# The out-projection as one level of Strassen's block scheme, after all merges, with the sums of w_out blocks formed on chip

## The chip, the core and the metric

The kernel runs on one core of one Trainium2 chip. The metric is the device time of one execution in microseconds; the kernel before took 2602.24 us, the median of three runs (2600.22 to 2603.6).

## What is computed

One decoder layer on 1024 tokens and 16 learned meta tokens, model width 2048, all in float32. An input projection feeds an attention branch and a pooling branch, each 1024 wide. What the change touches is the end, after the branches' outputs stand in DRAM:

```python
y_attn = o_attn @ w_attn_up          # (tokens, 1024) @ (1024, 2048)
y_pool = o_pool @ w_pool_up
merged = sigmoid(m_attn) * y_attn + sigmoid(m_pool) * y_pool
hs = x + merged @ w_out              # (tokens, 2048) @ (2048, 2048)
return rmsnorm(hs, final_gain)[:, N_META:]
```

## The kernel before

Matmuls of float32 accuracy are made of three: an operand is split into a high part in the type float32r (ScalarE, L116) and the rest (VectorE, L117), and high x high, high x low and low x high are accumulated in PSUM (`mm3`, and L910 to L912 in the out-projection). A weight tile is always 128 x 512. `load_w` (L127) loads it through SyncE's queue (SP, L124) into one of four raw buffers `wr` and splits it into one of four pairs `wh`, `wl`. So a weight tile is loaded when the split of the fourth one before it has been done, and split when TensorE (PE) has finished with the fourth one before it.

The tokens are worked in two halves of 512 (`t`). For each half there is first a **merge**: for 16 blocks `c` of 128 output columns, `up_mm` multiplies pooled and attention outputs by the two up-projections (24 matmuls and two weight tiles each), VectorE multiplies by the gate (`sp` L895, `sa` L901), GpSimd (POOL) adds the two (L902), and the sum is split into `m`, which stays on chip. Then comes the **out-projection** of the half, `out_pass`: all 16 blocks of `m` against w_out, four token blocks `b` and column blocks `c` of 512; each weight tile serves 4 x 3 = 12 matmuls. Residual, squares and the final gain follow (L945 to L957), and the rows are stored. So the order of stages is merge 0, out 0, merge 1, out 1. The attention outputs of the second half are loaded and split during out 0 (`fill_o`), into the place of the first half's. The last 512 columns of out 1 go by halves of 256 columns per token block, from weights split ahead (`lw`).

Which instruction stands where in an engine's queue is not the program's order: a scheduler sets it when the kernel is built. Each engine then works through its own queue in order, SP through its DMA issues too: an issue that waits for a semaphore holds all issues behind it. Before the first merge stands the input projection, itself by a block scheme, whose sums GpSimd forms and SP stores (`d_r`, L245), and the attention.

Of the kernel before, what the change touches and what calls it, by code (L numbers as in the profile page):

```python
# [15 lines left out]
P = 128  # L16
# [56 lines left out]
def trunk_kernel(  # L73
# [779 lines left out]

    def o_quads():
        return xquads(0, HALF, xo) + xquads(1, HALF, xo)

    def m_quads():
        return xquads(2, HALF) + xquads(3, HALF, xc)

    o = o_quads()  # L860
    for n in range(WID // P):
        fill_o(o, 0, n)

    psB = ctx.enter_context(tc.tile_pool(name="psB", bufs=8, space=bass.MemoryType.PSUM, reuse_waits="tile"))
    pb = ctx.enter_context(tc.tile_pool(name="pb", bufs=2, side="right", reuse_waits="tile"))
# [4 lines left out]
    def up_mm(w, o, c):  # L870
        a = acc_b()
        for q in range(2):
            whi, wlo = load_w(w_src(w, q, c * P))
            for j in range(QD):
                k = slice(j * P, (j + 1) * P)
                mm3(a, whi[:, k], wlo[:, k], o[q][0][:, j], o[q][1][:, j], q + j == 0, q == 1 and j == QD - 1)
        return a

    def merge(t, o, m):
        order = [("p", 0), ("p", 1), ("p", 2)] if t == 0 else []  # L880
        for c in range(KC):
            if ("p", c) not in order:
                order.append(("p", c))
            order.append(("a", c))
        sps = {}
        cs = slice(t * HALF, (t + 1) * HALF)
        for n, (kind, c) in enumerate(order):
            if t == 0 and n < 3:
                for i in range(WID // P + 3 * n, WID // P + min(3 * n + 3, 8)):
                    fill_o(o, 0, i)  # L890
            if kind == "p":
                sp = pb.tile([P, HALF], F32, tag="sp", name=nm("sp"), bufs=3)
                nc.sync.dma_start(sp, d_sp[c][:, cs])
                a = up_mm(w_pu, o[:2], c)
                nc.vector.tensor_tensor(out=sp, in0=a, in1=sp, op=ALU.mult)  # L895
                sps[c] = sp
            else:
                sa = pb.tile([P, HALF], F32, tag="sa", name=nm("sa"))
                nc.sync.dma_start(sa, d_sa[c][:, cs])
                a = up_mm(w_au, o[2:], c)  # L900
# [13 lines left out]
    def out_pass(m, cs, done, extra=None):  # L914
        accs = {(c, b): acc_b() for c in cs for b in range(HB)}
        groups = [(0, 1)] + [(k,) for k in range(2, KC - 2)] + [(KC - 2, KC - 1)]
        for ks in groups:
            if extra is not None:
                for k in ks:
                    extra(k)  # L920
            ws = {(c, k): load_w(w_out[k * P : (k + 1) * P, c * 512 : (c + 1) * 512]) for k in ks for c in cs}
            for (c, b), a in accs.items():
                for k in ks:
                    out_mm(a, m, b, k, *ws[c, k])
# [115 lines left out]
```

## Time and profile before

| | |
|---|---|
| median of 3 runs | 2602.24 us |
| the profiled execution | 2601.93 us, of which its span 2600.2 us |
| granted TensorE clock, mean | 0.986 |
| merge 0 | from 1883.4 us |
| out-projection 0 | from 2060.1 us |
| last 512-column matmul of out 1 | 2545.4 us |
| half-wide matmuls of out 1 | 2545.6 to 2591.6 us |
| DMA moved | 415.88 MB, mean 160 GB/s |

Times within the profile are microseconds from the start of the span. A window's line gives its length, then busy time and number of instructions of PE matmul, PE weight load, VectorE (DVE), ScalarE (ACT) and GpSimd, then the granted clock of PE, the busy share of the 16 DMA engines and what they moved in GB/s. A matmul's row shows its whole passage through the array; the next one starts before it ends, so the rate is read from counts in a window. In a line of a tile, the three numbers are the least, median and greatest ns of one instruction.

### The profile page before, as it was taken

Reading aid. Unit: us, or ns where it says so; the run is one execution under the profiler, and the core shown is the slowest. Engines: PE = TensorE matmul, PEld = TensorE weight load, DVE = VectorE, ACT = ScalarE, POOL = GpSimd, SP = SyncE. Lnnn points to the kernel's source line nnn. Section 1 sums busy time; section 2 is a strip of 40 time slices with the busy share of each in tenths; the row PEclk is TensorE's granted clock in tenths of the full one; section 3 lists DMA queues with packets and bytes.
Section 4 is the critical chain, followed back from the end, with each engine's and each line's share of the span. In section 5 each row is a group of like instructions: output and inputs, shape, how many; then the busy total and the mean of one; then the engine's idle time right before and its main releaser. Section 6 shows DMA issues by size and latency. Waiting matters only on the chain.

```text
span 2600.2 us, 36248 instructions
## 1 busy us (share of the span) xinstructions
PE 2502.7 (96%) x12968; PEld 2132.8 (82%) x12968; DVE 1279.1 (49%) x2121; ACT 930.7 (36%) x1893; POOL 873.3 (34%) x794
## 2 busy tenths in 40 slices
PE   6898999999999999899999999999899999999998
PEld 5776788888888887888888888888688888788888
DVE  5442345443334444675576567656644334544432
ACT  6421222222222234224454545454532223322331
POOL 1655555554455444233323332333111100211010
PEclk9999999999999999999999999999999999999999
DMA  5566555665555567434434443433385434664421
GB/s 180 168 213 209 198 196 201 208 225 183 176 187 184 172 192 233 125 127 137 128 122 130 129 126 122 135 124 98 128 265 146 139 101 146 203 185 142 150 98 65
DMA packets 392054, 415.88 MB, mean 160 GB/s; under 512 B 29873, under 2 KB 264753, under 8 KB 390833
## 3 DMA queue, kind: packets, MB, share of 16 engines
q1 hardware_dynamic: 391872, 413.57, 49.8%
q8 instruction: 101, 1.65, 0.3%
q14 instruction: 81, 0.66, 0.1%
HBM read 302.62 MB, written 110.85 MB: 159 GB/s over the span
## 4 chain that ended last, share of the span: by engine, by line
PE 82%; DVE 5%; DMA 3%; POOL 3%; issue 1%; ACT 1%; SPq 0%; POOLq 0%; DVEq 0%; ACTq 0%
PE acc L138 17%; PE acc L140 17%; PE acc L139 17%; PE accb L912 4%; PE accb L911 4%; PE accb L910 4%; PE accb L140 4%; PE accb L138 4%; PE accb L139 4%; POOL r L236 2%; DMA raw<-in_w_in_dram 2%; PE tr L730 1%; DVE s L658 1%; DVE wl L117 1%; DVE bt L715 1%
## 5 line engine op out<-in xcount | busy, mean ns | idle before, releaser
L138 PE MATMUL acc<-x,wh 128*128 128x512 f32 (+2 forms) x2736 | 980.4, 359 | 26.3 <-ACT wh L116 18.3
L140 PE MATMUL acc<-x,wl 128*128 128x512 f32 (+2 forms) x2736 | 971.0, 355 | 4.9 <-DVE wl L117 3.6
L139 PE MATMUL acc<-x,wh 128*128 128x512 f32 (+2 forms) x2736 | 970.0, 355 | 0.0
L138 PEld LDWEIGHTS acc<-x,wh 128*128 128x128 f32 x2736 | 520.1, 190 | 96.6 <-ACT wh L116 22.4
L140 PEld LDWEIGHTS acc<-x,wl 128*128 128x128 f32 x2736 | 519.0, 190 | 81.1 <-DVE wl L117 8.9
L139 PEld LDWEIGHTS acc<-x,wh 128*128 128x128 f32 x2736 | 519.8, 190 | 63.1
L116 ACT ACTIVATE wh<-wr 128x512 fp32r<-128x512 f32 x480 | 302.4, 630 | 522.0 <-PE accb L139 162.8
L117 DVE TENSOR_TENSOR wl<-wr,wh 128x512 fp32r<-128x512 f32 x360 | 257.8, 717 | 277.8 <-ACT wh L116 266.1
L117 DVE TENSOR_TENSOR wl<-r,wh 128x512 fp32r<-128x512 f32 x160 | 151.7, 951 | 309.5 <-ACT wh L116 303.6
L117 POOL TENSOR_TENSOR wl<-wr,wh 128x512 fp32r<-128x512 f32 x120 | 167.3, 1394 | 343.6 <-ACT wh L116 287.0
L116 ACT ACTIVATE wh<-r 128x512 fp32r<-128x512 f32 x160 | 100.4, 632 | 457.1 <-POOL r L236 333.5
L236 POOL TENSOR_TENSOR r<-raw,raw 128x512 f32<-128x512 f32 x80 | 112.3, 1403 | 375.1 <-DMA raw<-in_w_in_dram 339.3
L236 POOL TENSOR_TENSOR r<-r,raw 128x512 f32<-128x512 f32 x160 | 221.0, 1382 | 12.2 <-DMA raw<-in_w_in_dram 2.3
L138 PE MATMUL accb<-x,wh 128*128 128x512 f32 x512 | 201.3, 393 | 9.0 <-ACT wh L116 9.0
L140 PE MATMUL accb<-x,wl 128*128 128x512 f32 x512 | 201.0, 393 | 3.0 <-DVE wl L117 3.0
L139 PE MATMUL accb<-x,wh 128*128 128x512 f32 x512 | 200.8, 392 | 0.0
L912 PE MATMUL accb<-wl,x 128*128 128x512 f32 x448 | 174.4, 389 | 1.0 <-DVE wl L117 1.0
L910 PE MATMUL accb<-wh,x 128*128 128x512 f32 x448 | 174.3, 389 | 0.0
L911 PE MATMUL accb<-wh,x 128*128 128x512 f32 x448 | 174.3, 389 | 0.0
L117 DVE TENSOR_TENSOR wl<-raw,wh 128x512 fp32r<-128x512 f32 x136 | 110.2, 819 | 116.3 <-ACT wh L116 116.3
L714 DVE TENSOR_TENSOR_SCAN wt<-wt 128x272 f32<-128x272 f32 (+5 forms) x128 | 107.7, 842 | 110.0 <-POOL wt L709 64.7
L902 POOL TENSOR_TENSOR sa<-sa,sp 128x512 f32<-128x512 f32 x32 | 50.9, 1590 | 324.8 <-DVE sa L901 324.8
(166 smaller groups left out, 3032.0 us busy)
## 6 DMA issues: line engine op xcount, KB each, us to landing
raw<-in_w_in_dram SPq DMA_DIRECT2D x96, 512.0 KB, 5.9
d_r<-r SPq DMA_DIRECT2D x160, 256.0 KB, 2.0
wr<-d_r SPq DMA_DIRECT2D x160, 256.0 KB, 2.9
raw<-in_w_in_dram SPq DMA_DIRECT2D x152, 256.0 KB, 5.1
wr<-in_w_out_dram SPq DMA_DIRECT2D x128, 256.0 KB, 2.6
wr<-in_w_in_dram SPq DMA_DIRECT2D x80, 256.0 KB, 3.0
wr<-in_w_pool_up_dram SPq DMA_DIRECT2D x64, 256.0 KB, 3.9
wr<-in_w_attn_up_dram SPq DMA_DIRECT2D x64, 256.0 KB, 3.4
```

What stands on the lines that cost most here:

```text
L116: nc.scalar.activation(hi, src, AF.Copy)
L117: (eng or nc.vector).tensor_tensor(out=lo, in0=src, in1=hi.bitcast(F32), op=ALU.subtract)
L138: nc.tensor.matmul(ps, wh, rh, start=first, stop=False, skip_group_check=skip)
L139: nc.tensor.matmul(ps, wh, rl, start=False, stop=False, skip_group_check=skip)
L140: nc.tensor.matmul(ps, wl, rh, start=False, stop=last, skip_group_check=skip)
L236: nc.gpsimd.tensor_tensor(out=t, in0=a, in1=b, op=ALU.add)
L658: nc.vector.tensor_tensor(out=nxt[:, lo:], in0=cur[:, lo:], in1=cur[:, lo - sh : TOK - sh], op=ALU.add)
L714: nc.vector.tensor_tensor_scan(out=rev, data0=rev, data1=rev, initial=wt[:, w : w + 1], op0=ALU.mult, op1=ALU.bypass)
L902: nc.gpsimd.tensor_tensor(out=sa, in0=sa, in1=sps.pop(c), op=ALU.add)
L910: nc.tensor.matmul(a, sh, wh, start=k == 0, stop=False)
L911: nc.tensor.matmul(a, sl, wh, start=False, stop=False)
L912: nc.tensor.matmul(a, sh, wl, start=False, stop=k == KC - 1)
```

## The change

The out-projection of both halves becomes one product of 2 x 2 blocks: tokens in two halves, the 2048 inner channels in two (`kh`: 16 blocks of 128 as 2 x 8, `KH = 8`), and in each half of the columns (`p`) two blocks of 512 (`nh`). Seven block products take the place of eight. Each runs over `KH` weight tiles and both `p`, so 16 tiles; the last product's second half has its weights split ahead, as before.

Both merges now come first and store their result in DRAM (`d_m`). During merge 0 the operands of merge 1 are loaded (`fill_up` to `o1`); during merge 1 those of the first two products (`fill_a`). In each, eight calls of `w_forms` load four blocks of w_out (`w_block`; one of them twice), form four sums or differences with five GpSimd operations, and store them (`d_wf0` to `d_wf3`). Then the products run in the order A11, A12, R2, R3, R1, A22, R4. The sums of merged blocks (R2 and R3, R1 with the split of A22, R4) are made while earlier products run, one step after a weight tile: `m_tile` loads a block into one of two single buffers, `mr0` and `mr1`, `plus` adds on GpSimd, `put` splits. Products that several results use are copied to `s1` and added to rows, on GpSimd (24 additions) and VectorE.

The core of the diff (line numbers of names as L are the new file's from here on):

```diff
-    for t in range(2):
-        m = m_quads()
-        merge(t, o, m)
...
+    d_m = [dtile(f"d_m{c}", (P, SEQ)) for c in range(KC)]
+    d_wf = [[dtile(f"d_wf{n}_{p}", (P, KH * 512)) for p in range(2)] for n in range(4)]
...
+        def w_forms(p, j):
+            a, b, d, c = (pm.tile([P, 512], F32, tag=f"cw{i}", name=nm("cw")) for i in range(4))
+            for t, (kh, nh) in zip((a, b, d, c), ((0, 0), (0, 1), (1, 0), (1, 1))):
+                nc.sync.dma_start(t, w_block(p, j, kh, nh))
+            e = pm.tile([P, 512], F32, tag="cw4", name=nm("cw"))
...
+            op(e, b, c)
+            op(a, a, e)
+            nc.sync.dma_start(w_form(1)(p, j), e)
+            nc.sync.dma_start(w_form(0)(p, j), a)
+            a2 = pm.tile([P, 512], F32, tag="cw0", name=nm("cw"))
+            nc.sync.dma_start(a2, w_block(p, j, 0, 0))
+            op(b, b, a2)
+            op(d, d, c)
+            op(d, d, b, ALU.add)
+            nc.sync.dma_start(w_form(2)(p, j), b)
+            nc.sync.dma_start(w_form(3)(p, j), d)
...
+                    nc.gpsimd.tensor_tensor(out=sa, in0=sa, in1=sps.pop(c), op=ALU.add)
+                    nc.sync.dma_start(d_m[c][:, cs], sa)
+                if n > 3 and extras:
+                    extras.pop(0)()
...
+        for n in range(2 * WID // P):
+            extras.append(lambda n=n: fill_up(o1, 1, n))
+            if n % 2:
+                extras.append(lambda u=forms.pop(0): w_forms(*u))
+        merge(0, o, extras)
...
+    def prod(accs, A, src, first, step=None):
+        for j in range(KH):
+            wh, wl = load_w(src(j))
+            q, jj = divmod(j, QD)
+            for b, a in enumerate(accs):
...
+            if step is not None:
+                step()
+
+    def m_tile(i, j, t):
+        u = pr.tile([P, 512], F32, tag=f"mr{i}", name=nm("mr"), bufs=1)
+        nc.sync.dma_start(u, d_m[j][:, t * HALF : (t + 1) * HALF])
+        return u
+
+    def put(A, j, src):
+        q, jj = divmod(j, QD)
+        split(A[q][0][:, jj], A[q][1][:, jj], src)
+
+    def plus(u, v):
+        nc.gpsimd.tensor_tensor(out=u, in0=u, in1=v, op=ALU.add)
+
+    def make_r23(j):
+        u, v = m_tile(0, j, 0), m_tile(1, j, 1)
+        plus(u, v)
+        put(R3, j, u)
+        v = m_tile(1, KH + j, 1)
+        plus(v, u)
+        put(R2, j, v)
+
+    def make_r1(j):
+        u, v = m_tile(0, j, 1), m_tile(1, KH + j, 1)
+        put(A22, j, v)
+        plus(u, v)
+        put(R1, j, u)
+
+    def make_r4(j):
+        u = m_tile(0, j, 0)
+        for c, t in ((j, 1), (KH + j, 0), (KH + j, 1)):
+            plus(u, m_tile(1, c, t))
+        put(R4, j, u)
...
+    for p in range(2):
+        accs.append(group())
+        prod(accs[p], A11, lambda j: w_block(p, j, 0, 0), True, step)
...
+    for p in range(2):
+        prod(accs[p], A12, lambda j: w_block(p, j, 1, 0), False, step)
...
+            nc.gpsimd.tensor_tensor(out=hs, in0=hs, in1=s1[p, b], op=ALU.add)
...
+        prod(accs[p], R2, lambda j: w_form(0)(p, j), True, step)
...
+        prod(accs[p], R3, lambda j: w_form(1)(p, j), False, step)
...
+    load_rows(1, lambda b: big.tile([P, D], F32, tag=f"x2{b // 2}{b % 2}", name=nm("row")))
...
+        prod(a4, R1, lambda j: w_form(2)(p, j), True, step)
...
+        prod(a4, A22, lambda j: w_form(3)(p, j), True, step)
...
+    prod(a4, R4, lambda j: w_block(0, j, 1, 1), True, step)
```

Three places of the queues, as they stand in the built kernels. The first is SP in the middle of merge 0, around block 7 of 16. Before, it holds weight tiles of the up-projections (`wr`, two for each product) and gate tiles (`sp`, `sa`):

```order
L899 DMA sa_3774_19480<-d_sa7_95 128x512
L124 DMA wr_3786_19528<-in_w_pool_up_dram 128x4x128
L124 DMA wr_3789_19546<-in_w_pool_up_dram 128x4x128
L124 DMA wr_3794_19568<-in_w_attn_up_dram 128x4x128
L893 DMA sp_3798_19606<-d_sp9_113 128x512
L124 DMA wr_3797_19586<-in_w_attn_up_dram 128x4x128
```

Now, in the same merge, one call of `w_forms` stands there (`cw` blocks of w_out, `d_wf` its results), with a fill (`ol`) and a store of a merged block (`d_m`):

```order
L889 DMA cw_3776_19478<-in_w_out_dram 128x512
L889 DMA cw_3777_19479<-in_w_out_dram 128x512
L940 DMA d_m4_18779<-sa_3736_19286 128x512
L889 DMA cw_3778_19480<-in_w_out_dram 128x512
L889 DMA cw_3779_19481<-in_w_out_dram 128x512
L900 DMA cw_3781_19491<-in_w_out_dram 128x512
L936 DMA sa_3782_19498<-d_sa6_94 128x512
L124 DMA wr_3786_19503<-in_w_attn_up_dram 128x4x128
L897 DMA d_wf1_0_18793<-cw_3780_19486 128x512
L898 DMA d_wf0_0_18791<-cw_3776_19478 128x512
L904 DMA d_wf2_0_18795<-cw_3777_19479 128x512
L905 DMA d_wf3_0_18797<-cw_3778_19480 128x512
```

The second weight tile of that attention product, then eight more issues of weights, gates, fills and one merged block, and the next call's blocks follow:

```order
L124 DMA wr_3789_19521<-in_w_attn_up_dram 128x4x128
L873 DMA ol_3790_19540<-d_op6_86 128x512
L930 DMA sp_3791_19544<-d_sp7_111 128x512
L124 DMA wr_3795_19549<-in_w_pool_up_dram 128x4x128
L940 DMA d_m5_18780<-sa_3759_19392 128x512
```

The last place on SP is where R4 is made, during R3. Before, an out-projection's queue held weight tiles of w_out one after the other:

```order
L124 DMA wr_4551_23418<-in_w_out_dram 128x512
L124 DMA wr_4552_23446<-in_w_out_dram 128x512
L124 DMA wr_4555_23452<-in_w_out_dram 128x512
L124 DMA wr_4558_23458<-in_w_out_dram 128x512
L124 DMA wr_4559_23486<-in_w_out_dram 128x512
```

Now a load of a merged block (`mr<-d_m`) stands between any two of them, four for each step of R4; `d_wf1` is the weight form of R3:

```order
L1009 DMA mr_4548_23132<-d_m0_18775 128x512
L1009 DMA mr_4547_23130<-d_m0_18775 128x512
L124 DMA wr_4574_23238<-d_wf1_0_18793 128x512
L124 DMA wr_4581_23269<-d_wf1_0_18793 128x512
L1009 DMA mr_4549_23135<-d_m8_18783 128x512
L124 DMA wr_4588_23300<-d_wf1_0_18793 128x512
L1009 DMA mr_4550_23138<-d_m8_18783 128x512
L124 DMA wr_4595_23331<-d_wf1_0_18793 128x512
L1009 DMA mr_4555_23163<-d_m1_18776 128x512
```

Here `mr_4547` is the sum's buffer `mr0`; `mr_4548`, `mr_4549` and `mr_4550` follow each other in `mr1`, each after the addition of the one before.

On GpSimd, in the middle of R4, the additions of `s1` to the second half's rows (`row`, L1081) stand between the additions of R4 (L1017). Nothing like either was in the queue before, where GpSimd had one product with the final gain for each block of rows (L957):

```order
L1017 TENSOR_TENSOR mr_4575_23254<-mr_4575_23254,mr_4576_23256 128x512
L1081 TENSOR_TENSOR row_4625_23517<-row_4625_23517,s1_4369_22242 128x512
L1081 TENSOR_TENSOR row_4624_23512<-row_4624_23512,s1_4400_22396 128x512 x2
L1081 TENSOR_TENSOR row_4625_23517<-row_4625_23517,s1_4401_22398 128x512
L1017 TENSOR_TENSOR mr_4575_23254<-mr_4575_23254,mr_4577_23259 128x512
```

So the step's second addition moved behind four row additions.

324 lines of the change are left out of this document (194 added, 130 removed).

## The prediction

> **What bounds the kernel now.** I read the page's busy times first, then the windows of the last stage, then single tiles, then the timeline of each queue.
>
> ```profile
> PE 2502.7 (96%) x12968; PEld 2132.8 (82%) x12968; DVE 1279.1 (49%) x2121; ACT 930.7 (36%) x1893; POOL 873.3 (34%) x794
> core 0: us, PE busy (x) PEld busy (x) DVE busy (x) ACT busy (x) POOL busy (x), PEclk, DMA share, GB/s
> 1883.00:2060.00 177.00, 176.57 (x767) 145.88 (x768) 77.47 (x119) 53.04 (x87) 24.03 (x15) 0.98 0.63 190
> 2060.00:2240.00 180.00, 179.04 (x790) 147.88 (x789) 72.66 (x112) 64.12 (x119) 23.20 (x17) 1.00 0.37 120
> 2080.00:2130.00 50.00, 50.00 (x222) 41.39 (x222) 13.17 (x19) 11.38 (x18) 0.00 (x0) 1.00 0.29 95
> 2240.00:2290.00 50.00, 46.96 (x199) 38.05 (x198) 26.94 (x57) 12.68 (x23) 6.08 (x4) 0.97 0.93 298
> ```
>
> TensorE is the bound: merge (1883 to 2060) and out-projection (2060 to 2240) keep it busy 99 to 100% of their windows. In the steady stretch 2080 to 2130 it starts 222 matmuls in 50 us, one every 0.226 us, although a row prints 0.389 us for one, since they overlap. Only the change of halves (2240 to 2290) shows a gap: 199 starts where 222 fit.
>
> ```profile
> L910 PE MATMUL accb<-wh,x x448: 389/389/402, 2060.3 to 2544.9; 128*128 128x512 f32 x150
> L910 PE MATMUL accb<-x,x x128: 278/283/283, 2545.6 to 2591.3; 128*128 128x256 f32 x128
> 2103.82 0.63 ACT L116 ACTIVATE wh<-wr 128x512 fp32r<-128x512 f32 x1 [2.09 <-PE accb L911]
> 2106.54 0.63 ACT L116 ACTIVATE wh<-wr 128x512 fp32r<-128x512 f32 x1 [2.09 <-PE accb L911]
> 2107.20 0.69 DVE L117 TENSOR_TENSOR wl<-wr,wh 128x512 fp32r<-128x512 f32 x1 [2.03 <-ACT wh L116]
> wr<-in_w_out_dram SPq DMA_DIRECT2D x18, 256.0 KB, 2.5
> ```
>
> One weight tile feeds 12 matmuls; the cadence of its split is 2106.54 - 2103.82 = 2.72 us. A tile takes 2.5 us from issue to landing, 0.63 on ACT and 0.69 on DVE, and is ready about 4 us after its issue. ACT waits for PE here: four raw tiles and four split ones stand ready, so the queue leads PE by 7 or 8 tiles, some 20 us. That lead hides everything today, and it is what the change spends.
>
> **What it removes.** L910 to L912 issue 3 x 448 = 1344 wide and 3 x 128 = 384 half-wide matmuls. Seven block products instead of eight leave 13 x 8 x 12 = 1248 wide and 192 half-wide ones. 96 x 0.226 = 21.7 us; the half-wide ones take (2591.6 - 2545.6)/384 = 0.120 us, so 192 are 23.0. Together **-44.7**.
>
> At the change of halves 23 starts are missing, 5.2 us. In the new order the second half's operands are filled during the first merge, so this goes. The entry changes too:
>
> ```profile
> 1874.08 0.39 PE L140 MATMUL acc<-x,wl 128*128 128x512 f32 x1
> 1875.70 0.61 ACT L804 ACTIVATE st<-st 128x512 f32<-128x512 f32 x1
> 1883.43 0.79 PE L138 MATMUL accb<-x,wh 128*128 128x512 f32 x1 [8.96 <-ACT wh L116]
> ```
>
> PE waits 8.96 us for its first weights behind the fills. Now the weights are issued first, and the fills follow the last gate's store: 1876.3 + 0.4 + 2.5 + 1.3 = about 1880.7, 2.7 us earlier. Together **-8** (-3 to -10; the fills may pay it back).
>
> **What it adds in the merges.** Three up-products take PE 72 x 0.226 = 16.3 us. Beside them now stand 6 weight tiles, 3 gate tiles, 1.5 stores of merged blocks, 2 fills and the 9 transfers of one w_forms call: 21.5 x 262,144 bytes = 5.64 MB.
>
> ```profile
> 1890.00:1920.00 30.00, 30.00 (x134) 24.80 (x133) 15.32 (x24) 10.82 (x18) 3.35 (x3) 1.00 0.98 314
> L236 POOL TENSOR_TENSOR r<-r,raw 128x512 f32<-128x512 f32 x160 | 221.0, 1382 | 12.2 <-DMA raw<-in_w_in_dram 2.3
> 1966.45 0.34 SPq L899 DMA_DIRECT2D sa<-d_sa  x1
> 708.35 5.88 SPq L245 DMA_DIRECT2D d_r<-r  x3
> ```
>
> The DMA engines were 98% busy at 314 GB/s, 0.83 us a tile. So a group of three takes them 18.0 us at best, 1.7 more than PE needs. The order makes it worse in the first merge: the four d_wf stores stand together on SP, each behind a GpSimd result, and the second weight tile of the same product stands behind them. After the last store SP issues ten transfers, then the block loads; the fourth block is 15th in line, so it lands at 15 x 0.83 + 1.7 (2.5 less one tile's transfer) = 14.1 us. Five GpSimd operations of 1.38 follow: 14.1 + 6.9 = 21 us a form against 16.3. The row at 708.35 shows SP held so behind GpSimd sums. Seven intervals of 4.7 are 33, less some 8 us of lead at the first form: +25 (0 where issue at 0.42 us hides all, 40 with no lead). In the second merge the block loads are spread between weight tiles; only the engines' 1.7 x 8 = 14 stays, less 6 of lead: +8 (0 to 25). **+33**.
>
> The Trainium skill, "DMA: Bandwidth & Descriptors", in its section on measured bandwidth, gives 425 GB/s for a 16 MB transfer. By it a group of three would take 13.3 us, under PE's 16.3, and the merges would stay PE's. The trace speaks against it: 0.98 share at 314, 0.93 at 298, 0.29 at 95, so a full share is 320 to 328 at most.
>
> **What it adds in the products.** PE needs 2.72 us a tile. The sums of merged blocks (R2, R3, R1, A22, R4) go through two single buffers, mr0 and mr1, and their loads stand in SP's one queue between the weight tiles. A load waits until GpSimd or the split has released its buffer, and the weight tiles behind it wait too. The step costs are: load 2.5, add 1.38, put 0.63 + 0.69 + about 0.15 of handing over = 1.5, and 0.1 for each other hand-over.
>
> - R2 with R3: put 1.5, load 2.5, add 1.4, load 2.5, add 1.4 and hand-overs 0.3 = 9.6 us a step. It starts about 25 us after the first product (GpSimd has a row addition of the first copied sums ahead of it: 8 x 2.72 = 21.8). 27 tiles stand between its loads, 73 us of PE, against 8 x 9.6 + 5.5 for row additions = 82.
> - R1 with A22: add, put, load = 5.6 us a step, 45 against 14 tiles = 38. The lead carries most of both; I take 5 (0 to 20).
> - R4: put 1.5, three loads one after the other 7.5, three adds 4.1, hand-overs 0.6 = 13.7 us a step, 110 for eight. Sixteen row additions of GpSimd (22 us) stand among them, about half in the gaps of loads: 121. Between the 32 loads stand 32 weight tiles, 87 us of PE. **+34**.
>
> The fastest load and add that the trace shows bound this from below; a busy queue from above:
>
> ```profile
> L957 POOL TENSOR_TENSOR row<-row,fg x28: 1286/1297/1743, 2139.6 to 2547.4; 128x512 f32<-128x512 f32 x28
> DMA to landing us min/median/max: 2.1/3.5/6.3
> ```
>
> With 2.1 and 1.29 an R4 step is 12.2, 98 + 8 against 87, and the lead covers it: near 5. With the median 3.5 of the row tiles it is 16.7, 134 + 16: +63. I take the loads of the quiet window, since the new one is about half loaded: 8 transfers of 0.83 in 13.7 us. So **+39** (5 to 80).
>
> Splits of weights and blocks rise from 160 to 168, 0.63 us on ACT and 0.69 on DVE each; both engines idle over 60% of the window from 2060 to 2240, so they have no term. Row sums and final rows of the second half lie beside R4's product and the last 192 matmuls (45 us together); their sixteen DVE products are 12 us. If that cover went, 5 us.
>
> **Sum.** The profiled execution took 2601.9 us (span 2600.2 and 1.7 around it), 0.3 under the median 2602.2. 2601.9 - 44.7 - 8 + 33 + 39 = 2621. I say **2620**.
>
> **The rivals.**
> - *The lead holds, faster.* One mechanism: the weight queue. If an R4 step takes at most 4 x 2.72 = 10.9 us, or a step near 12 meets an intact lead of 20 us, SP reaches each weight tile before PE wants it; if a form also fits into 16.3, PE never waits and only the removed work counts: 2601.9 - 44.7 - 8 + 11 = 2560. For it: PE runs 99% through stages today in which SP is held by GpSimd for 5.88 us. Against: each link above is a measured one, and the sum is 13.7. Chance 0.18.
> - *The merges are free.* If the engines do not saturate, the fourth block lands at 15 x 0.42 + 2.5 = 8.8, the form ends at 15.7, under 16.3: 2621 - 33 = 2588. The Trainium skill ("DMA: Bandwidth & Descriptors", measured bandwidth) would have it so, as said above. Against: the 0.98 row. Chance 0.12.
> - *Loads are slow too.* Landing at 3.5 in the products, as the row tiles' median: 39 becomes 80, near 2660. Chance 0.13.
> - *The matmuls are not removed.* The new order lists 288 fewer rows on PE, which is 96 + 192; I give this nothing.
>
> **How the numbers follow.** The forecast has 0.57, most of it above the bound of no change. About 0.2% (5 us) is what a measurement of this kernel can tell from no change. The forecast's terms spread by some 20 us, so 0.09 of all falls within 2597 to 2607; the two faster cases have 0.30. Faster 0.30, same 0.09, slower 0.61. The range reaches from 2565, where the lead covers nearly all, to 2660, the slow loads; about half of each of those two cases lies beyond it, 0.15.
>
> **What would show it.** In the new profile: PE's busy time down by about 45 us, with its idle time up by some 65. In the first merge, windows of three up-products at 20 us with a DMA share above 0.85, PE waiting for splits that wait for up-projection weights, and SP waiting for GpSimd at the d_wf stores. In the products, R4's loads some 3.5 us apart, steps of 13 to 14 us, SP's longest waits at the mr loads, and PE idle in steps of 1 to 3 us. Products at a clean 2.72 us a tile through R3 and R1 refute the R4 term; a first merge of 177 us refutes the merge term. Entry later than 1883 or a gap between the two merges refutes the small one. I would be most wrong if the lead outlasts the chains, since then three terms fall together.

## The result, and the profile after

| | before | after |
|---|---|---|
| median | 2602.92 us (2600.22 to 2605.67, 4 runs) | 2691.74 us (2679.41 to 2693.79, 4 runs) |
| ratio | | 1.0331, 95% interval 1.0298 to 1.0365 |
| profiled execution, its span | 2601.93, 2600.2 | 2690.13, 2688.4 |
| mean granted TensorE clock | 0.986 | 0.968 |

The change makes the kernel 3.3% slower, 89 us, where the prediction said some 18 us and ended its range at 2660. The direction was right and the size was not. The first view is the page's busy times, then four windows: merge 0, merge 1, and the wide products cut where the first addition for R4 starts (2472.8).

```profile
PE 2512.8 (93%) x12680; PEld 2113.9 (79%) x12680; DVE 1336.1 (50%) x2153; ACT 932.4 (35%) x1909; POOL 1054.6 (39%) x930
1885.20:2107.10 221.90, 193.06 (x768) 154.02 (x769) 92.21 (x128) 59.25 (x96) 74.59 (x55) 0.91 0.81 258
2107.10:2311.60 204.50, 187.36 (x769) 149.00 (x768) 93.69 (x110) 45.13 (x78) 82.44 (x56) 0.95 0.77 247
2311.60:2472.80 161.20, 145.81 (x590) 114.34 (x589) 67.48 (x96) 55.75 (x105) 45.29 (x33) 0.95 0.53 173
2472.80:2656.40 183.60, 162.41 (x661) 129.22 (x660) 88.61 (x145) 52.78 (x106) 64.43 (x48) 0.93 0.53 178
```

The 288 matmuls are gone (12968 - 12680), yet PE's busy time rose by 10 us. Each window is to be held against its starts at 0.2265 us, the spacing that before showed in its steady stretch: 768 are 174 us, 590 are 134, 661 are 150. So merge 0 lost 48 us, merge 1 30.5, the products up to R4's first addition 27.5 and those behind it 34: 140 in all. The two merges' windows show 46.0 us of it as idle PE (28.8 and 17.1); the rest, 32 us, is matmuls that ran at a lower granted clock (0.91 and 0.95 in these windows). In the products it is 36.6 idle (344.8 less 145.81 and 162.41) and 25 slower. The timeline of PE in merge 0 shows how that comes (start, duration, and in brackets the idle time before and what ended it):

```profile
1990.53 0.39 PE L139 MATMUL accb<-x,wh 128*128 128x512 f32 x1
1990.76 0.39 PE L140 MATMUL accb<-x,wl 128*128 128x512 f32 x1
1994.17 0.66 PE L138 MATMUL accb<-x,wh 128*128 128x512 f32 x1 [3.03 <-ACT wh L116]
1994.63 0.63 PE L139 MATMUL accb<-x,wh 128*128 128x512 f32 x1
1995.06 0.64 PE L140 MATMUL accb<-x,wl 128*128 128x512 f32 x1
...
1997.20 0.63 PE L139 MATMUL accb<-x,wh 128*128 128x512 f32 x1
1997.63 0.47 PE L140 MATMUL accb<-x,wl 128*128 128x512 f32 x1
1997.93 0.40 PE L138 MATMUL accb<-x,wh 128*128 128x512 f32 x1
```

After 3.03 us of idle time the matmuls start 0.43 us apart for some 3.5 us, then again at the old spacing: this wait costs 3 us, and then 1.6 more (8 starts at 0.43 for 0.2265). Nearly all idle time of merge 0 is seven such waits of 3.0 to 5.1 us, about 23 us apart, one to a form, each with matmuls 0.43 us apart behind it. The Trainium skill, "TensorE: Matmul & The Clock Gate", Part 1, says that the clock halves after an idle window of about 3.4 us and needs about as long a busy one to come back. This trace agrees on the half and on the time back (3.5 us); a gap of 3.03 us (3.41 from start to start) was enough here. In merge 1 one of 1.91 us, ahead of the matmul at 2263.89, was followed by the wider spacing too, and one of 2.12 us, ahead of 2183.67, was not; so this trace gives no length below which a wait is safe.

What SP and ScalarE wait for in the merges, longest sums first (us in total, times, longest):

```profile
SPq L940 <- POOL sa L939: 50.4, 22, 5.0
SPq L897 <- POOL cw L893: 47.3, 15, 5.9
...
SPq L898 <- POOL cw L893: 28.4, 16, 2.6
SPq L904 <- POOL cw L893: 16.4, 12, 4.2
SPq L905 <- POOL cw L893: 14.3, 14, 1.4
```

```profile
ACT x L116 <- DMA ol<-d_m: 107.4, 14, 12.1
ACT wh L116 <- DMA wr<-in_w_attn_up_dram: 88.2, 30, 8.9
ACT wh L116 <- DMA wr<-in_w_pool_up_dram: 67.2, 21, 12.2
```

SP stands at the stores of forms, as was said (L897 to L905, 106 us), and about half as long (50) at the d_m store, which the prediction had not priced: its sum (L939) stands behind form operations in GpSimd's order. ScalarE waits 155 us for weight tiles, most of it in merge 0, and 107 for the fills in merge 1 (`ol<-d_m`), whose splits stand ahead of weight splits. In the products ScalarE waits longest for the sums of blocks:

```profile
ACT x L116 <- POOL mr L1017: 133.7, 32, 11.6
```

The landing times rose with the traffic:

```profile
cw<-in_w_out_dram SPq DMA_DIRECT2D x80, 256.0 KB, 5.7
mr<-d_m SPq DMA_DIRECT2D x72, 256.0 KB, 2.7
```

A block takes 5.7 us in the merges where 2.5 was the quiet window's; the products' loads take 2.7, as the forecast took them.

### The profile page after: what moved, and what is told of

Its sections match the earlier page's. It is cut to its first block, busy times and chain, and to the rows that moved or that the text cites. A ratio compares the mean times of both kernels' runs of the same rounds, so it can differ in the third digit from the quotient of the medians.

```text
span 2688.4 us, 36287 instructions
## 1 busy us (share of the span) xinstructions
PE 2512.8 (93%) x12680; PEld 2113.9 (79%) x12680; DVE 1336.1 (50%) x2153; ACT 932.4 (35%) x1909; POOL 1054.6 (39%) x930
## 4 chain that ended last, share of the span: by engine, by line
PE 58%; DMA 14%; POOL 10%; DVE 6%; issue 4%; ACT 2%; SPq 1%; POOLq 0%; DVEq 0%; ACTq 0%
PE acc L138 16%; PE acc L139 16%; PE acc L140 16%; DMA mr<-d_m 4%; POOL r L236 3%; POOL cw L893 3%; POOL mr L1017 2%; DMA raw<-in_w_in_dram 2%; DMA cw<-in_w_out_dram 2%; DVE wl L117 1%; DMA ol<-d_m 1%; PE tr L730 1%; DVE s L658 1%; ACT x L116 1%; DVE x L117 1%
## 5 line engine op out<-in xcount | busy, mean ns | idle before, releaser
L138 PE MATMUL acc<-x,wh 128*128 128x512 f32 (+2 forms) x2736 | 981.0, 359 | 24.7 <-ACT wh L116 15.8
L116 ACT ACTIVATE wh<-wr 128x512 fp32r<-128x512 f32 x472 | 292.1, 628 | 470.0 <-PE acc L139 174.5
L117 DVE TENSOR_TENSOR wl<-wr,wh 128x512 fp32r<-128x512 f32 x352 | 284.8, 819 | 264.2 <-ACT wh L116 258.4
L138 PE MATMUL accb<-x,wh 128*128 128x512 f32 x512 | 211.2, 413 | 45.2 <-ACT wh L116 37.1
L236 POOL TENSOR_TENSOR r<-r,raw 128x512 f32<-128x512 f32 x160 | 226.5, 1416 | 12.4 <-DMA raw<-in_w_in_dram 2.5
L140 PE MATMUL accb<-x,wl 128*128 128x512 f32 x512 | 209.9, 410 | 8.7 <-DVE wl L117 8.5
L139 PE MATMUL accb<-x,wh 128*128 128x512 f32 x512 | 209.3, 409 | 0.0
L1000 PE MATMUL accb<-wh,x 128*128 128x512 f32 x416 | 170.6, 410 | 25.4 <-ACT wh L116 25.4
L1001 PE MATMUL accb<-wh,x 128*128 128x512 f32 x416 | 168.5, 405 | 0.0
L893 POOL TENSOR_TENSOR cw<-cw,cw 128x512 f32<-128x512 f32 x80 | 112.5, 1430 | 121.1 <-DMA cw<-in_w_out_dram 120.0
```

The lines of the kernel that those rows point to most:

```text
L116: nc.scalar.activation(hi, src, AF.Copy)
L117: (eng or nc.vector).tensor_tensor(out=lo, in0=src, in1=hi.bitcast(F32), op=ALU.subtract)
L138: nc.tensor.matmul(ps, wh, rh, start=first, stop=False, skip_group_check=skip)
L139: nc.tensor.matmul(ps, wh, rl, start=False, stop=False, skip_group_check=skip)
L140: nc.tensor.matmul(ps, wl, rh, start=False, stop=last, skip_group_check=skip)
L236: nc.gpsimd.tensor_tensor(out=t, in0=a, in1=b, op=ALU.add)
```

## Experiments

Each kernel is the kernel after with one edit, unless said otherwise. "Merges" is the time from the first up-product to the first wide product, "products" from there to the first half-wide matmul, read from the starts of the rows of `accb`. At 0.2265 us a start they would be 348 and 283. Except for the last two of the section "Together" each was run once, with no interval, and they ran on five chips; the kernel before took 2596 to 2606 us beside them. How far single runs spread shows in stages that an edit left alone: merges like those of the kernel after read 425.1 to 429.3 us, products 340.1 to 346.2. A difference of some 5 us is not read as an effect.

| kernel | total | merges | products |
|---|---|---|---|
| after | 2691.7 | 426.7 | 344.7 |
| e1 no forms | 2611.65 | 351.3 | 344.0 |
| e2 forms copied | 2648.73 | 380.6 | 345.9 |
| e6 form stores from GpSimd | 2691.34 | 430.4 | 344.7 |
| e8 merged sum on VectorE | 2679.22 | 421.4 | 343.4 |
| e8b both | 2675.80 | 416.9 | 343.8 |
| e11 and fills split on GpSimd | 2678.98 | 417.5 | 343.6 |
| e17 forms on VectorE, eight transfers | 2642.83 | 383.8 | 341.7 |
| e21 forms on VectorE, nine transfers | 2659.95 | 390.1 | 346.2 |
| e22 forms on GpSimd, eight transfers | 2696.10 | 433.4 | 340.1 |
| e4 R4 from R2 | 2671.09 | 428.0 | 326.3 |
| e10 sums asked for further apart | 2692.02 | 429.0 | 339.8 |
| e5 loads of blocks from GpSimd | 2723.47 | 425.2 | 380.8 |
| e12 whole sums on GpSimd | 2756.96 | 429.3 | 410.0 |
| e14 e11 with e12 | 2730.32 | 406.2 | 407.0 |
| e15 sums on VectorE | 2641.14 | 425.1 | 301.8 |
| e18 e15, e17, e4 | 2613.09 | 385.1 | 306.8 |
| e19 e15, e17, merged sum on VectorE | 2595.79 | 374.8 | 302.2 |
| e20 e19, d_m stores from GpSimd | 2608.51 | 388.1 | 298.9 |

### What the forms cost: e1 and e2

e1 leaves `w_forms` out, and the products read plain blocks of w_out in place of the forms (so that part of the result is not formed):

```diff
-        return lambda p, j: d_wf[n][p][:, j * 512 : (j + 1) * 512]
+        return lambda p, j: w_block(p, j, n // 2, n % 2)
...
-            if n % 2:
-                extras.append(lambda u=forms.pop(0): w_forms(*u))
```

> The sixteen calls of w_forms are left out, with their 144 transfers and 80 GpSimd operations; the products read plain blocks of w_out instead, so the output is not the reference's. Merges with fills and stores of merged blocks, without forms. If the forms are what the merges lose (both the queue theory and the engine theory), the two merges take 355 to 365 us instead of 426 and the total is near 2625. If fills, d_m stores and the splits standing behind them in ScalarE's queue cost on their own, the merges stay above 380.

e2 keeps the nine transfers of a form and leaves out the five operations: blocks are stored as loaded, so the forms hold plain blocks.

```diff
-            op(e, b, c)
-            op(a, a, e)
-            nc.sync.dma_start(w_form(1)(p, j), e)
+            nc.sync.dma_start(w_form(1)(p, j), c)
...
-            op(b, b, a2)
-            op(d, d, c)
-            op(d, d, b, ALU.add)
```

> The five GpSimd operations of each w_forms call are left out and the loaded blocks are stored as they are: the same 9 transfers a call, no wait for GpSimd; the output is not the reference's. Queue theory (weight tiles stand behind stores that wait for GpSimd): a form falls from 23 us to about 17, the merges to 360 to 375 us, total near 2635. Engine theory (the DMA engines are near full and loads land late in whatever order): the merges stay above 400 us, total above 2665.

The window of all merges, first of e1, then of e2:

```profile
1882.80:2234.10 351.30, 351.30 (x1536) 290.34 (x1537) 160.48 (x238) 105.54 (x174) 48.76 (x31) 0.99 0.64 199
```

```profile
1888.70:2269.10 380.40, 363.10 (x1535) 294.17 (x1536) 166.19 (x238) 105.92 (x174) 46.03 (x31) 0.97 0.89 284
```

Without forms PE never waits: 351 us, so the fills, the d_m stores and the order of splits cost next to nothing by themselves. The forms are all of the 75 us. Their transfers alone cost 29 (the DMA share is 0.89 then); the other 46 go with the GpSimd operations. e2's 380.6 lies between its two theories' ranges.

### Which wait is it: e6, e8, e8b, e11

e6 issues the four stores of a form from GpSimd, so that SP no longer stands at them:

```diff
-            nc.sync.dma_start(w_form(1)(p, j), e)
+            nc.gpsimd.dma_start(w_form(1)(p, j), e)
```

> Only the four d_wf stores of each form are issued from GpSimd's own queue instead of SP's; work and transfers are those of the changed kernel. Queue theory: SP is no longer held behind GpSimd, merges at most 385 us, total near 2645. Engine theory: about 420 us, total above 2675. If GpSimd's issuing is itself slow, the forms get longer and the merges exceed 426.

Nothing was gained (430.4). SP's waits in the merges of e6:

```profile
SPq L940 <- POOL sa L939: 108.7, 26, 8.3
...
SPq L889 <- POOL cw L893: 24.1, 11, 5.5
SPq L889 <- DMA d_wf<-cw: 13.4, 4, 4.8
```

The hold at the form stores, 106 us of waits in the kernel after, became a hold at the d_m store. So that sum went to VectorE, alone (e8) and with e6's edit (e8b):

```diff
-                    nc.gpsimd.tensor_tensor(out=sa, in0=sa, in1=sps.pop(c), op=ALU.add)
+                    nc.vector.tensor_tensor(out=sa, in0=sa, in1=sps.pop(c), op=ALU.add)
```

> The addition that makes a merged block (sa + sp) runs on VectorE instead of GpSimd; nothing else changes. Both earlier readings leave about 46 us of the merges' 426 to waits for GpSimd. Theory A: the d_m store is what counts, since its sum stood behind form operations in GpSimd's own order. Then SP's waits at L940 for GpSimd (54 us) vanish, nothing replaces them, merges 380 to 400, total 2645 to 2665. Rival B: either of two holds is enough (the stores of the forms hold SP just as long when the d_m store doesn't). Then the waits move to the form stores L897 to L905, merges 415 to 430, total 2680 to 2692.

> The addition of the merged blocks on VectorE and the forms' stores issued by GpSimd itself: SP waits for GpSimd nowhere in the merges except where a block is loaded into a cw buffer whose form isn't stored yet. Same transfers, same operations. If SP's holds make the 46 us (theory A or B of the other run), merges come to 375 to 395 as with copied forms (380), total 2640 to 2660; the transfers' 29 us stay. Rival C: the chain of one form (block loads, five operations, stores, buffers free) sets the period by itself through the cw buffers: SP waits at L889 instead, over 60 us of it, merges 410 to 430.

e8 came out as rival B had it by its length (421.4), but the waits at the form stores stayed where they were (109 us) and did not grow. e8b came to 416.9, in the range of rival C, yet not for its reason: the stores at L905 stand 17.0 us apart in the first merge, where they stood 23.2 apart, so a form's own chain does not set the pace there. SP's longest wait is now for a raw buffer of its own weight tiles (129.8 us at L124), which VectorE's part of a split frees. SP no longer waited for GpSimd's sums and PE waited nonetheless. ScalarE in e8b, in a stretch of merge 0:

```profile
2001.03 1.36 ACT L116 ACTIVATE x<-ol 128x512 fp32r<-128x512 f32 x2 [7.35 <-DMA ol<-d_oa]
2002.30 1.66 ACT L116 ACTIVATE wh<-wr 128x512 fp32r<-128x512 f32 x3
2004.67 0.63 ACT L116 ACTIVATE wh<-wr 128x512 fp32r<-128x512 f32 x1 [0.71 <-DVE x L117]
2017.18 1.29 ACT L116 ACTIVATE x<-ol 128x512 fp32r<-128x512 f32 x2 [11.89 <-DMA ol<-d_oa]
2018.38 1.66 ACT L116 ACTIVATE wh<-wr 128x512 fp32r<-128x512 f32 x3
```

ScalarE stands 11.89 us ahead of a fill's split, and three weight tiles that lie there ready are split in one row behind it. So e11 takes the fills' splits off ScalarE, on top of e8b (both parts on GpSimd; the entry's fills stay):

```diff
+    def split_pool(hi, lo, src):
+        nc.gpsimd.tensor_copy(hi, src)
+        nc.gpsimd.tensor_tensor(out=lo, in0=src, in1=hi.bitcast(F32), op=ALU.subtract)
```

> As e8b_sa_dve_wf_pool (total 2675.8, merges 416.5, SP free of GpSimd), and the splits of the fills made during the merges (second half's operands, merged blocks of the first half) run on GpSimd, both parts, in place of ScalarE and VectorE. Theory D: what is left is ScalarE's own order: a fill's split stands ahead of weight splits and waits for its late load (98 us of such waits between 1890 and 2240 in e8b). Then weight tiles are split as they land, merges 365 to 390, total 2625 to 2650. Rival E: the DMA engines (0.91 busy in the first merge) deliver the weight tiles themselves too late; then ScalarE waits for weights instead of fills, merges 400 to 418, total above 2660. Nothing changes in the products.

417.5, by its length as rival E had it: theory D falls as the whole cause. ScalarE has no fill left in the merges' middle, but the weight tiles land late (171 us of waits), and VectorE's part of the weight splits (between 1890 and 2130 us) now takes 1366 ns on average where it took 924 in e8b, 838 in the kernel after and 688 in the one before. The edit also gives GpSimd more to do, so it does not try ScalarE's wait alone. Why shows best in e14, where GpSimd is fullest; VectorE, then GpSimd, in the same stretch:

```profile
2004.23 0.68 DVE L940 TENSOR_TENSOR sa<-accb,sa 128x512 f32<-128x512 f32 x1
...
2006.81 7.29 DVE L121 TENSOR_TENSOR wl<-wr,wh 128x512 fp32r<-128x512 f32 x1
2014.02 0.68 DVE L934 TENSOR_TENSOR sp<-accb,sp 128x512 f32<-128x512 f32 x1
```

```profile
2007.34 2.52 POOL L117 TENSOR_TENSOR x<-ol,x 128x512 fp32r<-128x512 f32 x2
2009.83 3.72 POOL L897 TENSOR_TENSOR cw<-cw,cw 128x512 f32<-128x512 f32 x3
2013.50 0.56 POOL L902 DMA_DIRECT2D d_wf<-cw  x1
```

A weight split of 0.69 us takes 7.29, until after GpSimd's row of operations has ended; the operations with one operand in PSUM (`accb`) keep their 0.68. The Trainium skill, "SBUF — State Buffer", section "SBUF: two separate sides", says that VectorE and GpSimd share a pair of ports under an exclusive lock, which a VectorE operation needs where both its inputs lie in SBUF. The trace agrees; the page holds the loser back for one instruction, and here it stood through all five of GpSimd's.

So there are three waits beside each other: SP behind GpSimd, ScalarE behind late fills, VectorE behind GpSimd's hold on the operands. Taking away the first moved PE's waiting rather than ended it. In the merges PE waited 37 us for ScalarE's part of a weight split and 8.5 for VectorE's in the kernel after, 19 and 24 in e8b, 16 and 26 in e11. What the three have in common is GpSimd's operations and loads that land late. That each alone would be long enough was not tried. In e8b the forms also came closer together and the DMA share of the first merge rose from 0.81 to 0.91; how much of its waiting is that, no run separates.

### The engine itself: e17, e21, e22

```diff
-                nc.gpsimd.tensor_tensor(out=out, in0=x0, in1=x1, op=alu)
+                nc.vector.tensor_tensor(out=out, in0=x0, in1=x1, op=alu)
...
             op(e, b, c)
+            op(b, b, a)
             op(a, a, e)
...
-            a2 = pm.tile([P, 512], F32, tag="cw0", name=nm("cw"))
-            nc.sync.dma_start(a2, w_block(p, j, 0, 0))
-            op(b, b, a2)
```

e17 has both parts of this diff, e21 the first alone, e22 the second alone.

> The form operations run on VectorE, and each form loads its first block once (eight transfers, not nine); form stores on SP and the merged blocks' sum on GpSimd as in the kernel after. In e11 and e14 VectorE's splits of two SBUF operands took up to 7.3 us while GpSimd worked through its operations, so GpSimd held PE there in a third way. Theory J: with GpSimd out of the forms neither that nor SP's long waits at the stores remain, and the forms stand evenly over both merges: 370 to 392, total 2635 to 2658, near e2's 380. Rival K: the in-order hold moves once more, to VectorE, whose weight splits then stand behind form operations waiting for late blocks: 405 to 430, total above 2668.

> Only the engine of the five form operations changes, GpSimd to VectorE; all nine transfers of a form stay. e17 changed both (merges 383.8). If the engine is what counts: merges 384 to 396, total 2645 to 2660. If the second load of the first block counts as much (it keeps a cw buffer and SP waiting): 400 to 420, total above 2662.

> Only the second load of each form's first block is left out (eight transfers; the operations in an order that needs no second copy); the operations stay on GpSimd. A ninth of the transfers' 29 us would be 3, so with the engine as the cause: merges 418 to 426, total 2683 to 2692. If the second load was what held the form up: 395 to 415, total below 2680.

The window of all merges in e21:

```profile
1889.90:2280.00 390.10, 368.39 (x1536) 293.31 (x1537) 212.19 (x318) 104.85 (x174) 48.49 (x31) 0.97 0.87 276
```

The engine alone gives 37 us (426.7 to 390.1), the ninth transfer alone nothing (433.4, even 7 more and above both its ranges), both together 43. e21 stands within 10 us of e2, which does no operations at all. SP still waits 52.6 us for the d_m sums in e21, so that wait by itself does not bring the loss; moving that sum to VectorE as well took off another 9 us (383.8 in e17, 374.8 in e19 below). An operation takes 0.69 us on VectorE where it took 1.29 on GpSimd. Five of them save 3 us of a form's chain, 48 us over sixteen forms, which is more than the 37 that came off. So the shorter chain could be all of it; but the late splits, the holds behind them and the half-clock matmuls shrink with it, and in e8b, where forms followed each other faster still, only 10 us came off. How the 46 us divide among these in the kernel after was not separated.

### The products: e4, e10, e5, e12, e15

e4 stores R2's sum when it is made, and R4 is that sum and one block, two loads and one addition for four and three:

```diff
+        nc.sync.dma_start(d_r2[j], v)
         put(R2, j, v)
...
-        u = m_tile(0, j, 0)
-        for c, t in ((j, 1), (KH + j, 0), (KH + j, 1)):
-            plus(u, m_tile(1, c, t))
+        u = m_tile(0, KH + j, 0)
+        v = pr.tile([P, 512], F32, tag="mr1", name=nm("mr"), bufs=1)
+        nc.sync.dma_start(v, d_r2[j])
+        plus(u, v)
```

> The sum that R2 is split from is stored once (8 stores), and R4 is made from it and one merged block: two loads and one addition a step instead of four loads and three additions in a chain. Chain theory for the products: R4's step falls from 15.3 us (with row additions) to 6 to 8, the products from 368 us to 335 to 345, total near 2662. If the products are held by something else (granted clock, the splits' queue, row loads), they stay above 358 and the total above 2680.

The products lost 18.4 us of their 344.7, less than expected: R4 is not all of it. e10 changes only the places at which steps are asked for:

```diff
-    step = stepper([lambda j=j: make_r4(j) for j in range(KH)])
+    step = r4_step = stepper(spaced([lambda j=j: make_r4(j) for j in range(KH)], 5))
```

> Only the places change at which the sums of merged blocks are asked for in the products: R2 with R3 at every fourth weight tile instead of each of the first eight, R1 at every second, R4 at every fifth from the start of R3's product on (up to and through R1's and A22's), the last fills at every second. In SP's order the loads for R2 and R3 move little (27 tiles before, 29 after), those of R4 from 32 tiles to some 41. Theory: an R4 step of 15.3 us stands against four tiles, 10.9 us, in the kernel after, and against five, 13.6, here, so products shrink from 345 to 315-330, total 2660 to 2677. Rival: the lead is gone after R2/R3 and R1, whose spacing stays, and R4's waits only move: over 335, total above 2680.

339.8, the rival's, and hardly outside the spread of products that no edit touched. The step of R2 with R3 takes 10.9 us there, as in the kernel after (11.0): a step that is asked for later is not a shorter one. e5 issues the blocks' loads from GpSimd, e12 puts every link of a sum on GpSimd:

```diff
-        nc.sync.dma_start(u, d_m[j][:, t * HALF : (t + 1) * HALF])
+        nc.gpsimd.dma_start(u, d_m[j][:, t * HALF : (t + 1) * HALF])
...
-        split(A[q][0][:, jj], A[q][1][:, jj], src)
+        split_pool(A[q][0][:, jj], A[q][1][:, jj], src)
```

> The loads of merged blocks in the products (32 + 16 + 24 rows at L1009) are issued from GpSimd's queue instead of SP's, so weight tiles on SP stand behind none of them. The sums' own chains stay as long, or grow by 0.56 us for each issue. Theory: SP's hold at these loads (166 us of waits) is what starves PE; then PE waits only where a sum comes too late for its own product, and products shrink from 345 to 295-320, total 2640 to 2668. Rival: ScalarE's and VectorE's order holds the weight tiles just as long, since the splits of the sums stand among those of the weights (134 us of ScalarE waits for GpSimd's sums): 330 to 350, total above 2675.

> In the products all links of the sums (loads, additions, both parts of the splits) are on GpSimd and its queue, so that SP, ScalarE and VectorE serve weight tiles alone. In e5_mr_pool only the loads were moved, and it was slower (products 380 for 345). Theory F: a step of the sums holds the weight tiles through whichever in-order queue it shares with them; then PE waits only where a whole operand comes late, wide products 290 to 315, total 2637 to 2662. Rival G: the chains themselves are too slow for their products (R2 with R3 eight steps of 11 us or more against 87 us of PE, now with 2.8 us for a split on GpSimd): the wait stands in one piece ahead of the product with R2 and of R4, 325 to 370. Merges as in the kernel after, 426.

Both are slower, each beyond the range of its own rival (380.8 and 410.0). PE's longest waits in the products of e12, and VectorE's:

```profile
PE accb L1004 <- ACT wh L120: 73.0, 2, 51.6
PE accb L1006 <- DVE wl L121: 26.7, 2, 24.7
```

```profile
DVE row L993 <- POOL row L1085: 78.6, 4, 58.7
```

PE stops twice, for 51.6 and 24.7 us, as VectorE's row sums wait for GpSimd's row additions, which stand behind the sums of blocks. SP had run far ahead (it waits up to 86 us for a raw buffer) and it helped nothing. So in e12 the length of GpSimd's chain is the bound, not SP's place in it. To try that in the kernel after, e15 shortens the links and leaves loads and splits where they are: `plus` and the two groups of row additions go to VectorE.

```diff
-        nc.gpsimd.tensor_tensor(out=u, in0=u, in1=v, op=ALU.add)
+        nc.vector.tensor_tensor(out=u, in0=u, in1=v, op=ALU.add)
...
-            nc.gpsimd.tensor_tensor(out=hs, in0=hs, in1=s1[p, b], op=ALU.add)
+            nc.vector.tensor_tensor(out=hs, in0=hs, in1=s1[p, b], op=ALU.add)
```

> In the products the additions of merged blocks and the two groups of row additions of copied sums move from GpSimd to VectorE (0.69 us for 1.38); loads, splits and merges as in the kernel after. Theory H: the length of the sums' chains sets the products' pace, since e12_sums_pool with longer links took 410 us for 345. Each addition saves 0.7 us on the chain and the row additions leave it: R2/R3 10.8 to 9.4 us a step, R4 15.3 to 12 or so, products 300 to 320, total 2646 to 2668. Rival I: VectorE's own order now holds the weight splits behind additions that wait for loads: 338 to 370, total above 2683.

301.8, inside theory H's range. The first addition of the first and of the eighth step of R2 with R3, in the kernel after and in e15:

```profile
2334.05 1.29 POOL L1017 TENSOR_TENSOR mr<-mr,mr 128x512 f32<-128x512 f32 x1 [0.24 <-DMA wr<-in_w_out_dram]
...
2411.38 1.29 POOL L1017 TENSOR_TENSOR mr<-mr,mr 128x512 f32<-128x512 f32 x1 [5.01 <-DMA mr<-d_m]
```

```profile
2327.56 0.69 DVE L1017 TENSOR_TENSOR mr<-mr,mr 128x512 f32<-128x512 f32 x1 [0.90 <-DMA mr<-d_m]
...
2392.82 0.69 DVE L1017 TENSOR_TENSOR mr<-mr,mr 128x512 f32<-128x512 f32 x1 [3.08 <-DMA mr<-d_m]
```

A step went from 11.0 us ((2411.38 - 2334.05)/7) to 9.3; in the same way R1's from 6.4 to 5.5 and R4's from 15.3 to 14.1. Eight of each make some 31 us, and 43 came off the products. PE's granted clock over the products rose with it, from 0.94 to 0.98, which fits the other 12. What the sums and what the row additions give was not tried apart.

### Together: e14, e18, e19, e20

e14 joins e11 and e12 with the first block loaded once.

> The two runs before together (merged sums on VectorE, form stores, fills and all sums of the products on GpSimd), and each form loads its first block once instead of twice (eight transfers for nine; the operations in another order). If theories D and F hold, merges 360 to 385 and products 290 to 315, total 2570 to 2610: level with the kernel before or better. If rival E or G holds, total 2630 to 2670.

Its merges are 406.2, its products 407.0, its total 60 us above the range that the rivals were given (2630 to 2670): GpSimd is worse as a place for this work than either rival had it. A window in its first merge:

```profile
1935.00:1985.00 50.00, 44.42 (x193) 35.79 (x192) 47.50 (x25) 9.49 (x15) 49.91 (x52) 1.00 1.01 337
```

GpSimd is busy all the time, and VectorE needs 47.50 us for 25 operations, 1.9 us each.

e18 joins e15, e17 and e4:

> e15 and e17 together, and R4 made from the stored sum R2 and one block (e4_r4short, which gave 19 us). If H and J hold: merges 370 to 392, products 290 to 310, total 2580 to 2615, level with or below the kernel before (2602). If one of the rivals holds, 2625 to 2660; if both, above 2670.

2613.09, inside the range: e15 gave 51 us and e17 49, and e18 gives 79 of these 99. R4 from the stored R2 does not help any more (306.8 for e15's 301.8). So e19 leaves it out and puts the merged sum (L939) on VectorE too; e20 besides issues the d_m stores from GpSimd's queue, empty by then.

> e15 and e17 together, R4 from four blocks as in the kernel after (in e18 the stored R2 made the products 5 us longer than in e15), and the merged blocks' sum on VectorE too, so that SP waits less at the d_m stores (57 us in e18). Merges 372 to 385, products 298 to 306, entry 1880 to 1888: total 2595 to 2612. If the sum on VectorE only holds VectorE's splits, merges 385 to 395 and total 2608 to 2622.

> As e19_lean, with the d_m stores issued from GpSimd's queue, which has nothing else to do here: SP waits in the merges only for the form operations on VectorE, and runs further ahead with the weight tiles. What is left is the transfers, 29 us in e2 with nine for a form, here with eight: merges 360 to 378, total 2585 to 2603. If the engines are then as full as the weight tiles can stand (the forms stand in the first three quarters of the merges here), merges 378 to 392, total 2603 to 2618.

e19: 2595.79 us, median of nine runs (2584.06 to 2603.59, and one of 4931.1 whose cause is not known and which is left out of the comparison); ratio to the kernel before 0.9968, interval 0.9950 to 0.9987. e20: 2608.51, 1.0019 (1.0009 to 1.0030). The windows of merges and products in e19:

```profile
1881.40:2256.20 374.80, 359.58 (x1537) 287.80 (x1537) 217.39 (x349) 103.12 (x175) 0.00 (x0) 0.99 0.87 276
2256.20:2558.40 302.20, 289.05 (x1249) 234.93 (x1248) 188.10 (x310) 108.64 (x210) 10.93 (x8) 0.98 0.59 198
```

With GpSimd out of both stages the seven products beat the eight by 0.3%: 27 us of loss are left in the merges and 19 in the products, against 45 of matmuls saved and some 7 at the seams. Freeing SP further (e20) made the merges 13 us longer, against the theory that SP's hold was what is left; 388.1 lies in the range expected if the engines are as full as the weight tiles can stand. The scheduler set its forms a little earlier (the last store at 2179 us, in e19 at 2195); whether that is the cause no run tried.

## Why the prediction was right or wrong

- **Removed work, right.** 288 matmuls are gone from the trace, and the half-wide ones take 23.0 us (2656.6 to 2679.6) where they took 46.0. In e19 their 45 us come out, less the losses that are left there. The change of halves' gap is gone too.
- **Entry, wrong by 4.5 us.** The first up-product starts at 1885.2, not at 1880.7. Among kernels that hardly differ there it lies between 1880.3 (e15) and 1889.9 (e21), so this small term was not the forecast's to know.
- **First merge, 48 us for 25.** The mechanism was right here: PE waits seven times for ScalarE's part of a weight split, ScalarE waits for weight tiles (some 125 us between 1920 and 2090, and under 8 for fills), and SP stands at the form stores. The step "14.1 + 6.9 = 21 us a form" was near: the stores at L905 stand 23.2 us apart. What failed is the size of the sum: 2.2 us more a form make 15, and "less some 8 us of lead at the first form" was not there. The prediction's own seven intervals with the measured step and no lead are 7 x (23.2 - 16.3) = 48. By PE's rows the same 48 are 28.8 of waits, near the 25, and 19 of matmuls at the lower granted clock behind them, which no term held. Whether these lengthened the step, or filled time in which PE would have waited for it anyway, no run separates.
- **Second merge, 30.5 us for 8.** The step was that "the block loads are spread between weight tiles; only the engines' 1.7 x 8 stays". The engines were not what bound it (share 0.77), and its period was 22.9 us for the predicted 18. e2 gives the transfers 29 us over both merges; GpSimd's part, which the prediction took to be nothing here, was there: SP waited 46 us at the form stores and 18 at the d_m store (2110 to 2300), and ScalarE 107 us for fills whose splits stand ahead of weight splits, against 27 for weight tiles. How the 30.5 divide among these was not tried.
- **R2, R3 and R1, 27.5 us for 5.** The chains were sized nearly right (11.0 for 9.6, 6.4 for 5.6): from 2334.05 to 2472.84 they ran 139 us, 12 more than the 127 summed. "The lead carries most of both" failed: by the starts PE lost all that the chains lacked, and the 20 us of lead paid nothing. The prediction gave the splits "no term", as ScalarE and VectorE idle over half the time. It is their order that counts: ScalarE's 133.7 us of waits show that a sum's split stands ahead of weight splits, so raw tiles that lie behind it are no lead. e5 took the loads off SP and the products grew by 36 us, but its loads then stand in GpSimd's own order. That ScalarE's order is the whole reason was not tried apart.
- **R4, right.** 34 us said and 34 lost; the step was 15.3 us, 121/8 = 15.1 was predicted. e4 shows that a shorter R4 gives 18 of it back.
- **The rivals.** That the lead holds did not come true in the kernel after and comes nearest in e15's products. "Merges free" needs forms without GpSimd and without their transfers (e1). The one on slow loads had its mechanism in the wrong stage: block loads took 5.7 us in the merges, and 2.7 in the products, where it put them. The rate of 425 GB/s that the prediction weighed from the Trainium skill, "DMA: Bandwidth & Descriptors", was not met, nor did the prediction's own bound of 328 hold: e14 moved 337 GB/s in a window of 50 us at a full share.
- **What would show it.** Named rightly: the SP waits at the d_wf stores and periods over 20 us in the first merge; PE's idle time rose by 78 us, near the 65. R4's steps were named as 13 to 14 us and took 15.3. The entry later than 1883, a named refutation of the small term, came. Named wrongly: PE's busy time would fall by 45; it rose by 10, since matmuls behind a wait ran slower. The DMA share in merge 0 was 0.81, not above 0.85.

The error in one line: waits were added up as if one queue were held at a time, with a lead in hand that paid for part of it. The largest part of the loss hangs on GpSimd doing the added operations: on VectorE 37 of the merges' 79 us (e21) and 43 of the products' 62 (e15) came back. The transfers of the forms are the next (e2).

## What to carry to other kernels

Where a new stage adds two-operand operations beside a stream of weight splits, ask first which engine runs them: on GpSimd they were slow links here, and they held VectorE's operations on SBUF as well. If freeing a queue gains nothing, look for another wait beside it and for what the two share, and take that away, rather than the next wait. And price a wait of PE above its length: in the kernel after 83 us of idle time came with 57 us of slower matmuls.

## What the runs showed of the hardware beside that

A GpSimd instruction that issues a DMA kept that engine 0.54 to 0.56 us (the row at 2013.50), where most of SP's issues in the kernel after took 0.32 to 0.43. Loads of 256 KB took 4.5 to 5.6 us at the median in merge 0 of the kernel after, at a DMA share of 0.81, about twice the 2.5 of the quiet window before.
